# RWKV time mixing on one core: when output tiles are stored and when their buffers are used again

## The chip, the core and the metric

The kernel runs on one core of one Trainium2 chip. The time is the device time of one execution in microseconds, as a median over runs. The profile is of one execution and gives its span, which is a little shorter than the time of the same run (286.8 us of 288.48 us).

## The reference

The inputs are `k` and `v` of shape 16 x 2048 x 256 (batch, time, channel) and per-channel vectors `w` and `u`, all float32. For every batch and channel a state `(aa, bb, pp)` is carried over time:

```python
ww = u + kk
qq = np.maximum(pp, ww)
e1 = np.exp(pp - qq)
e2 = np.exp(ww - qq)
output[b, t, :] = (e1 * aa + e2 * vv) / (e1 * bb + e2 + 1e-08)
ww = pp - w + kk
qq = np.maximum(ww, kk)
e1 = np.exp(ww - qq)
e2 = np.exp(kk - qq)
aa = e1 * aa + e2 * vv
bb = e1 * bb + e2
pp = qq
```

`aa` and `bb` are a decayed sum of `exp(k) v` and of `exp(k)`; `pp` is a running maximum that keeps the exponentials in range. Each output is a quotient of two such sums. Both inputs have to be read once and the output written once: 67.12 MB read and 33.55 MB written.

## The kernel before, in words

**Tiles.** Time is cut into 16 chunks of 128 steps (`NST`), and the 16 batches into 4 groups of four. That gives 64 tiles (`NP`), numbered `n = 4 * chunk + group`. A tile of `k`, of `v` or of the output is 128 partitions (the steps) by 4 batches by 256 channels in float32, 512 KB, and is moved by one DMA.

**One slot.** The main loop (lines 458 to 497) handles one tile per pass, which is called a slot here; slots 0 to 9 run a shorter loop (lines 425 to 445). In slot `n`

- `exps(n)` (L222) lets ScalarE take the exponentials that TensorE prepared in PSUM (`logs`, L203 and L209);
- `round_k(n + 2)` (L193) and `cast_v` (L227) let VectorE copy a loaded `k` or `v` tile into its working form, and give its float32 load buffer back;
- `times_v(n)` (L233) multiplies by `v`;
- for the tile `q = n - 10` (`LAG` is 10), TensorE makes the denominators (`den`, L360), and ScalarE turns them into reciprocals in a float32 output buffer `RD[q]`: `den_log` (L365, a logarithm), then `den_exp` (L368);
- for `qp = n - 11`, TensorE makes the numerators (`num`, L377), and VectorE multiplies them into the same buffer (`mult`, L381). The tile is then complete.

**The state across chunks** is worked on once in four slots, on small tiles: `sums`, `copy_sums`, `turn`, `state_logs`, `state_frames`, `state_scan` (a scan on VectorE, L292), `state_offsets` (L301 to L305), `state_weights` (an exponential on ScalarE, L309), `state_chain`, and `inject`, which writes the new state into the operand ring `EZR` with four small DMAs (L350). `state_offsets(c)` has five element-wise instructions of at most 128 x 64 elements. `E` is the engine of the first three: VectorE in chunks 0, 1 and 15 (`ON_DVE`), GpSimd else. `E2` is the engine of the last two: GpSimd in all chunks but the last.

**Buffers.** All 512 KB tiles share 19 buffers (`BUFS`). At the start 8 of them (`OUTS`) are in the list `free_out`, for outputs, and 11 in the list `free`, for loads. Each entry has the slot from which it may be taken, and `take` takes the earliest. `store(n, slot)` (L385) puts the stored buffer back into `free_out` with the slot `slot + STORED`, and `den_log` takes one there. If fewer than three output buffers will be available in two slots, `loads` moves a load buffer over to the outputs, for good (line 81). `loads` issues `v` and `k` loads (L73, L69), at most nine tiles ahead, while two load buffers are free; with fewer load buffers it gets less far ahead.

**Order.** The order of the instructions on each engine is written out by hand: `K` keeps them in program order. All loads and all stores go through the one queue of SyncE (called SPq in the profile) in program order, and an entry there that waits for its buffer holds back all behind it. Where an instruction takes a buffer before its store has landed, the build adds a wait. The slot numbers of `take` only decide which buffer is taken; they do not make anything wait.

**How late stores are.** In slot `n` the last complete tile is `qp - 1`, with `qp = n - 11`. While loads are left to issue, line 485 allows stores of tiles below `qp - 2 - max(0, n - 18) // 6`: two slots later than possible at first, three from slot 24, and one more every six slots, until they are eight late at slot 54. In each slot in which this number steps, no store is issued. When all loads are issued, the held-back stores go out at once: nine in slot 60. Loads get the bandwidth that the held-back stores leave.

Of the kernel before, what the change touches and what calls it, by code (L numbers as in the profile page):

```python
# [10 lines left out]
ALU = mybir.AluOpType  # L11
# [4 lines left out]
def kernel(  # L16
# [9 lines left out]
    K = tc.keep_in_program_order  # L26
    PE, DVE, SC, POOL, SP = nc.tensor, nc.vector, nc.scalar, nc.gpsimd, nc.sync
# [6 lines left out]
    NP = 4 * NST  # L34
    RING = 12
    BUFS, OUTS = 19, 8
    STORED = 3
    LAG = 10
    RS = 2.0 ** -20
    CAP = 54.0  # L40
# [11 lines left out]
    def rows_of(x, n):  # L52
        c, p = divmod(n, 4)
        return x[4 * p:4 * p + 4, c * TC:(c + 1) * TC, :].rearrange("n t d -> t n d")
# [22 lines left out]
    loaded = 5  # L77

    def loads(slot):
        nonlocal loaded  # L80
        if slot + 2 >= LAG and sum(x <= slot + 2 for x, _ in free_out) < 3:
            free_out.append((slot + 2, take(slot, free)))
        while loaded < NP and loaded - slot < 9 and sum(x <= slot for x, _ in free) >= 2:
            load_v(loaded, slot)
            loaded += 1
            if loaded < NP:
                load_k(loaded, slot)
# [102 lines left out]
    def round_k(n, slot=0):  # L190
        km = consts.tile([128, 4, Dm], F32R, tag=f"km{n % 2}", name="km") if n < 2 else KM[n - 2]
        kr = kr_of.pop(n)
        K(DVE.tensor_copy(km, kr))  # L193
        free.append((slot, kr))
        KM[n] = km

    def logs(n):
        km = KM[n].rearrange("p (i n) d -> p i (n d)", i=2)

        def rows(q):  # L200
            for i in range(2):
                g = 32 * (2 * q + i)
                K(PE.matmul(half(n, q)[:, i, :], CO[g:g + 32, :],  # L203
                            WU[g:g + 32, :].unsqueeze(1).broadcast_to([32, 2, Dm]), start=True, stop=False,
                            tile_position=(g, 0), skip_group_check=True))

        def steps(q):
            for i in range(2):
                K(PE.matmul(half(n, q)[:, i, :], (NLE, NLZ)[q], km[:, i, :], start=False, stop=True,  # L209
                            skip_group_check=True))  # L210

        rows(0)
        rows(1)
        steps(0)
        steps(1)

    def exps(n):
        if n < TURNS:
            for q in range(2):
                K(SC.activation(ez(n)[:, q], half(n, q), ACT.Exp))  # L220
        else:
            K(SC.activation(ez(n)[:, 0:2], PS[:, 0:4, :].rearrange("p (q i) x -> p q i x", q=2), ACT.Exp))  # L222

    def cast_v(n, slot=0):
        vb = vbpool.tile([128, 4, Dm], BF16, tag="vb", name="vb")
        vr = vr_of.pop(n)
        K(DVE.tensor_copy(vb, vr))  # L227
        free.append((slot, vr))
        VB[n] = vb

    def times_v(n):
        vb = VB.pop(n).rearrange("p (i n) d -> p i (n d)", i=2)
        K(DVE.tensor_mul(ez(n)[:, 2:4], ez(n)[:, 0:2], vb.unsqueeze(1).broadcast_to([128, 2, 2, D])))  # L233
# [61 lines left out]
    def state_offsets(c):  # L295
        E = DVE if c in ON_DVE else POOL
        E2 = POOL if c < NST - 1 else DVE
        A, P, F = [x[c % 2] for x in (A_of, P_of, F_of)]
        out = A.rearrange("p h m -> p m h")
        Q = tiny.tile([128, 32, 2], F32, tag="Q", name="Q")  # L300
        K(E.tensor_tensor(Q, P[:, :, 0:2], F[:, :, 1:3], ALU.add))  # L301
        K(E.tensor_tensor(out[:, :, 0:2], Q, P[:, :, 1:3], ALU.subtract))
        K(E.tensor_single_scalar(out[:, :, 2:4], Q, CAP, op=ALU.min))
        K(E2.tensor_single_scalar(out[:, :, 4:6], P[:, :, 1:3], -1.0, op=ALU.mult))
        K(E2.tensor_copy(LL_of[(c + 1) % 2][:, 0, :, 0:1], P[:, :, 2:3]))  # L305

    def state_weights(c):
# [49 lines left out]
    def den(n, bank=DENB):  # L357
        for m, q in (("L", 0), ("Id", 1)):
            for i in range(2):
                K(PE.matmul(bank[:, i, :], mats[m], ez(n)[:, q, i, :], start=q == 0, stop=q == 1,  # L360
                            skip_group_check=True))
# [13 lines left out]
    def num(n, bank, i):  # L375
        for m, q in (("LN", 2), ("IdN", 3)):
            K(PE.matmul(bank, mats[m], ez(n)[:, q, i, :], start=q == 2, stop=q == 3, skip_group_check=True))  # L377

    def mult(n, bank, i):
        rd = RD[n]  # L380
        K(DVE.tensor_mul(rd[:, i, :], bank, rd[:, i, :]))  # L381

    def store(n, slot):
        rd = RD.pop(n).rearrange("p i (n d) -> p (i n) d", n=2)
        K(SP.dma_start(out=rows_of(out, n), in_=rd))  # L385
        free_out.append((slot + STORED, rd))

    later = {}
    for c in range(NST):
        s = 4 * c + 3  # L390
        plan = [(s + 1, "act" if s + 1 < LAG else "recip", copy_sums), (s + 1, "pe", turn),
                (s + 2, "act", state_logs), (s + 2, "mid", state_frames), (s + 2, "scan", state_scan), (s + 2, "scan", state_offsets),
                (s + 3, "recip", state_weights), (s + 3, "chain", state_chain),
                (s + 4, "nums", turn_back), (s + 4, "mid", inject), (s + 4, "mid", state_next)]
        if c == 0:
            plan = [(s + 1, "act", copy_sums), (s + 1, "pe", turn), (s + 1, "pe", state_logs),
                    (s + 1, "round", state_frames), (s + 1, "round", state_scan), (s + 1, "round", state_offsets),
                    (s + 2, "act", state_weights), (s + 2, "round", state_chain),
                    (s + 3, "pe", turn_back), (s + 3, "round", inject), (s + 3, "round", state_next)]
        if c == 1:  # L400
            plan = [(s + 1, "act", copy_sums), (s + 1, "pe", turn), (s + 2, "act", state_logs),
                    (s + 2, "round", state_frames), (s + 2, "round", state_scan), (s + 2, "round", state_offsets),
                    (s + 3, "recip", state_weights), (s + 3, "early", state_chain)] + plan[8:]
        if c == NST - 1:
            plan = []
        for slot, where, f in plan:
            later.setdefault((slot, where), []).append((f, c))

    def small_work(n, where):
        for f, c in later.pop((n, where), []):  # L410
            f(c)
# [35 lines left out]
    stored = 0  # L447

    def inverses(n):
        q, qp = n - LAG, n - LAG - 1  # L450
        if qp >= 0:
            num(qp, NUMB, 1)

        sums(n - 1)
        if n + 1 < NP:
            recip(q, lambda: small_work(n, "recip"))

    for n in range(LAG, NP):

        q, qp = n - LAG, n - LAG - 1  # L460
        if qp >= 0:
            num(qp, NUMB, 0)
        den(q)
        small_work(n, "nums")
        exps(n)
        small_work(n, "act")
        if qp >= 0:
            mult(qp, NUMB, 0)
        small_work(n, "mid")
        if n == LAG:  # L470

            inverses(n)
            small_work(n, "early")
        if n + 2 < NP:
            round_k(n + 2, n)

        if n % 4 in (3, 0):
            cast_v(n, n)
        if n + 1 == NP:
            times_v(n)  # L480
        elif n % 4 < 2:
            cast_v(n + 1, n)
        loads(n)

        while stored < (qp - 2 - max(0, n - 18) // 6 if loaded < NP else qp):
            store(stored, n)
            stored += 1
        if n > LAG:
            inverses(n)
        if qp >= 0:  # L490
            mult(qp, NUMB, 1)
        small_work(n, "scan")
        if n + 1 < NP:
            times_v(n)
            small_work(n, "chain")
            logs(n + 1)
        small_work(n, "pe")
# [53 lines left out]
    n, p = NP - 1, (NP - 1) % 4  # L551
# [38 lines left out]
```

## Time and profile before

| what | value |
|---|---|
| time, median of 3 runs | 289.18 us (288.41 to 289.48) |
| span of the profiled execution | 286.8 us |
| TensorE matmul busy | 261.9 us (91%) |
| VectorE busy | 261.0 us (91%) |
| ScalarE busy | 254.0 us (89%) |
| GpSimd busy | 104.3 us (36%) |
| moved by DMA | 101.54 MB, mean 354 GB/s |
| 512 KB loads and stores, median from issue to landing | 8.0, 8.2 and 7.8 us (`k`, `v`, output) |

Three engines are near 90% busy and the DMA is nearly full too, so no single share tells what bounds the kernel. The stretches have to be read one by one: the first 40 us, in which tiles are loaded and nothing is stored; the slots from about 52 us to 254 us; and the last 33 us, in which only outputs are finished.

### The profile page before, as it was taken

Reading aid. Unit: us, or ns where it says so; the run is one execution under the profiler, and the core shown is the slowest. Engines: PE = TensorE matmul, PEld = TensorE weight load, DVE = VectorE, ACT = ScalarE, POOL = GpSimd, SP = SyncE. Lnnn points to the kernel's source line nnn. Section 1 sums busy time; section 2 is a strip of 40 time slices with the busy share of each in tenths; the row PEclk is TensorE's granted clock in tenths of the full one; section 3 lists DMA queues with packets and bytes.
Section 4 is the critical chain, followed back from the end, with each engine's and each line's share of the span. In section 5 each row is a group of like instructions: output and inputs, shape, how many; then the busy total and the mean of one; then the engine's idle time right before and its main releaser. Section 6 shows DMA issues by size and latency. Waiting matters only on the chain.

```text
span 286.8 us, 5076 instructions
## 1 busy us (share of the span) xinstructions
PE 261.9 (91%) x1694; PEld 119.5 (42%) x1694; DVE 261.0 (91%) x463; ACT 254.0 (89%) x252; POOL 104.3 (36%) x208
## 2 busy tenths in 40 slices
PE   6998896999999999699999999999999999997980
PEld 2444442544444444344444344444454444533430
DVE  4699989999999999699999999999999999987771
ACT  2586768999999998799999999999999999996990
POOL 7000524362535454143445445253445454340000
PEclk9999999999999999999999999999999999999997
DMA  6999999999999999999999999999999999999797
GB/s 220 355 348 349 348 329 349 332 348 355 385 376 383 383 383 373 382 383 379 375 379 377 372 371 384 322 383 371 360 304 380 367 333 370 379 383 369 230 340 253
DMA packets 103586, 101.54 MB, mean 354 GB/s; under 512 B 4284, under 2 KB 103560, under 8 KB 103560
## 3 DMA queue, kind: packets, MB, share of 16 engines
q1 hardware_dynamic: 101336, 100.45, 103.8%
q0 software_dynamic: 1920, 0.50, 0.8%
q8 instruction: 13, 0.21, 0.3%
q10 hardware_dynamic: 304, 0.27, 0.3%
q14 instruction: 13, 0.11, 0.1%
HBM read 67.12 MB, written 33.55 MB: 351 GB/s over the span
## 4 chain that ended last, share of the span: by engine, by line
DVE 38%; PE 21%; DMA 16%; ACT 12%; issue 10%; DVEq 1%; POOL 0%; ACTq 0%; POOLq 0%
DVE EZR L233 15%; DVE buf L381 11%; PE PS L209 8%; PE PS L377 7%; DMA buf<-in_k_dram 6%; DMA out_dram<-buf 6%; ACT buf L368 4%; DVE km L193 4%; ACT buf L365 4%; DVE vb L227 3%; PE PS L203 3%; PE PS L257 3%; ACT EZR L222 2%; DMA EZR<-cb 2%; DMA wuf<-in_u_dram 2%
## 5 line engine op out<-in xcount | busy, mean ns | idle before, releaser
L222 ACT ACTIVATE EZR<-PS 128x2048 bf16<-128x2048 f32 x54 | 101.2, 1875 | 3.6 <-PE PS L209 2.6
L381 DVE TENSOR_TENSOR buf<-PS,buf 128x512 f32<-128x512 f32 x128 | 86.9, 687 | 8.0 <-ACT buf L368 3.6
L233 DVE TENSOR_TENSOR EZR<-EZR,vb 128x2048 bf16<-128x2048 bf16 x64 | 78.2, 1222 | 2.9 <-ACT EZR L220 2.3
L365 ACT ACTIVATE buf<-PS 128x1024 f32<-128x1024 f32 x64 | 65.9, 1029 | 4.6 <-DMA out_dram<-buf 2.8
L368 ACT ACTIVATE buf<-buf 128x1024 f32<-128x1024 f32 (+1 forms) x65 | 67.8, 1048 | 0.9
L350 POOL DMA_DIRECT2D EZR<-cb x60 | 36.8, 619 | 53.2 <-DVE cb L345 46.5
L377 PE MATMUL PS<-EZR,LN 128*128 128x512 bf16 x128 | 48.8, 381 | 6.8 <-DVE buf L381 2.5
L209 PE MATMUL PS<-km,NLE 128*128 128x512 f32 x128 | 47.6, 454 | 1.5 <-DVE km L193 1.5
L377 PE MATMUL PS<-EZR,IdN 128*128 128x512 bf16 x128 | 48.4, 378 | 0.0
L193 DVE CAST km<-buf 128x1024 fp32r<-128x1024 f32 x64 | 43.9, 686 | 1.4 <-DMA buf<-in_k_dram 1.3
L227 DVE CAST vb<-buf 128x1024 bf16<-128x1024 f32 x64 | 43.2, 691 | 0.3 <-DMA buf<-in_v_dram 0.3
L209 PE MATMUL PS<-km,NLZ 128*128 128x512 f32 x128 | 41.0, 403 | 0.0
L360 PE MATMUL PS<-EZR,L 128*128 128x512 bf16 x128 | 38.1, 379 | 1.8 <-DMA EZR<-cb 1.6
L360 PE MATMUL PS<-EZR,Id 128*128 128x512 bf16 x128 | 38.1, 379 | 0.0
L288 POOL TENSOR_TENSOR F<-LL,LL 128x32 f32<-128x32 f32 x13 | 8.2, 631 | 65.5 <-ACT LL L279 65.5
L203 PE MATMUL PS<-WU,CO 32*128 32x512 bf16 x256 | 26.9, 392 | 2.5 <-DVE WU L421 1.6
L257 PE MATMUL PS<-EZR,OH 128*32 128x256 bf16 x512 | 26.2, 277 | 1.1 <-ACT LL L279 1.0
L209 PEld LDWEIGHTS PS<-km,NLZ 128*128 128x128 f32 x128 | 24.6, 192 | 5.7
L220 ACT ACTIVATE EZR<-PS 128x1024 bf16<-128x1024 f32 x20 | 19.4, 1019 | 8.1 <-PE PS L209 8.1
L209 PEld LDWEIGHTS PS<-km,NLE 128*128 128x128 f32 x128 | 19.4, 191 | 16.7 <-issue 13.4
L377 PEld LDWEIGHTS <-IdN 128*128 128x128 bf16 x128 | 12.5, 97 | 22.3 <-issue 20.2
L377 PEld LDWEIGHTS <-LN 128*128 128x128 bf16 x128 | 12.8, 100 | 18.4 <-issue 11.3
(71 smaller groups left out, 201.6 us busy)
## 6 DMA issues: line engine op xcount, KB each, us to landing
buf<-in_k_dram SPq DMA_DIRECT2D x64, 512.0 KB, 8.0
buf<-in_v_dram SPq DMA_DIRECT2D x64, 512.0 KB, 8.2
out_dram<-buf SPq DMA_DIRECT2D x63, 512.0 KB, 7.8
EZR<-cb POOLq DMA_DIRECT2D x60, 8.0 KB, 5.4
out_dram<-buf SPq DMA_DIRECT2D x2, 128.0 KB, 4.4
out_dram<-buf ACTq DMA_DIRECT2D x2, 128.0 KB, 4.5
EZR<-cb SPq DMA_DIRECT2D x4, 8.0 KB, 3.7
wuf<-in_w_dram ACTq DMA_DIRECT2D x1, 8.0 KB
```

Of the source, the lines that this page charges most:

```text
L193: K(DVE.tensor_copy(km, kr))
L203: K(PE.matmul(half(n, q)[:, i, :], CO[g:g + 32, :], WU[g:g + 32, :].unsqueeze(1).broadcast_to([32, 2, Dm]), start=True, stop=False, tile_p ...
L209: K(PE.matmul(half(n, q)[:, i, :], (NLE, NLZ)[q], km[:, i, :], start=False, stop=True, skip_group_check=True))
L222: K(SC.activation(ez(n)[:, 0:2], PS[:, 0:4, :].rearrange("p (q i) x -> p q i x", q=2), ACT.Exp))
L227: K(DVE.tensor_copy(vb, vr))
L233: K(DVE.tensor_mul(ez(n)[:, 2:4], ez(n)[:, 0:2], vb.unsqueeze(1).broadcast_to([128, 2, 2, D])))
L350: K(queue.dma_start(out=EZR[r:r + 1, 2 * q, r0:r0 + 4, :, :].rearrange("o p i (b x) -> o (p i b) x", b=4), in_=cb[x:x + 32, :]))
L360: K(PE.matmul(bank[:, i, :], mats[m], ez(n)[:, q, i, :], start=q == 0, stop=q == 1, skip_group_check=True))
L365: K(SC.activation(RD[n], bank, ACT.Ln, scale=RS))
L368: K(SC.activation(RD[n][:, i, :], RD[n][:, i, :], ACT.Exp, scale=-1.0))
L377: K(PE.matmul(bank, mats[m], ez(n)[:, q, i, :], start=q == 2, stop=q == 3, skip_group_check=True))
L381: K(DVE.tensor_mul(rd[:, i, :], bank, rd[:, i, :]))
```

## The change

The change moves stores earlier, gives a stored buffer more time before it is used again, and moves two small instructions:

1. `STORED` goes from 3 to 4: a buffer is offered to `den_log` four slots behind its store in place of three.
2. The holding back of stores begins at slot 20 and steps every twelve slots: stores are two slots late up to slot 31, three from 32, four from 44 and five from 56. The number of held-back stores at the end is smaller, six being issued in slot 59.
3. In `state_offsets`, the negation (line 304) goes where the first three instructions are. That differs from before in chunks 0 and 1, where it moves from GpSimd to VectorE.

By the pools' rule, the first edits also change which load buffers go over to the outputs: before, one each in slots 31, 37, 43, 49 and 55; after, one each in slots 34 and 58. So more buffers are left for loads in the second half.

```diff
-    STORED = 3
+    STORED = 4
...
-        K(E2.tensor_single_scalar(out[:, :, 4:6], P[:, :, 1:3], -1.0, op=ALU.mult))
+        K((E if E is DVE else E2).tensor_single_scalar(out[:, :, 4:6], P[:, :, 1:3], -1.0, op=ALU.mult))
...
-        while stored < (qp - 2 - max(0, n - 18) // 6 if loaded < NP else qp):
+        while stored < (qp - 2 - max(0, n - 20) // 12 if loaded < NP else qp):
             store(stored, n)
             stored += 1
```

The instructions of TensorE and ScalarE stay the same and in the same order. VectorE gets two instructions more and GpSimd two fewer. On SyncE the same 170 issues stand in another order.

## The prediction

> **What bounds the kernel now.** I read the windows first, cut at starts of the large exponential (L222), which stands once in each slot: slots 18 to 27, 28 to 37 and 38 to 62. The columns are the stretch and its length, busy time of each engine, granted clock, DMA share and GB/s.
>
> ```profile
> core 0: us, PE busy (x) PEld busy (x) DVE busy (x) ACT busy (x) POOL busy (x), PEclk, DMA share, GB/s
> 71.95:111.66 39.71, 38.83 (x261) 17.72 (x260) 39.26 (x67) 39.21 (x38) 18.46 (x34) 1.00 1.09 381
> 111.66:154.54 42.88, 39.16 (x261) 18.17 (x260) 40.01 (x65) 39.67 (x38) 15.44 (x33) 1.00 1.09 380
> 154.54:253.60 99.06, 96.96 (x650) 44.73 (x649) 97.45 (x162) 98.10 (x95) 43.90 (x83) 1.00 1.06 362
> ```
>
> The first ten slots take 39.71 us, the last 25 take 99.06 us: 3.97 and 3.96 us each, with three engines over 96% busy. That is the pace of compute. The ten slots between take 42.88 us for the same work, 3.2 us more than ten times 3.97. The reader should also see the last column. While every slot stores a tile, it moves three tiles of 524,288 bytes; from the first row's 381 GB/s that is 1.573 MB / 381 = 4.13 us, more than 3.97. The DMA is slightly slower than compute there. Late in the run, where before stores only five tiles in six slots, it idles: (381 - 362) GB/s over 99 us is 1.9 MB, 3.6 tiles.
>
> Next the waits, to see who stopped in the slow stretch (total us, times, longest):
>
> ```profile
> DVE buf L381 <- ACT buf L368: 3.6, 7, 0.7
> ...
> DVE buf L381 <- PE PS L377: 3.1, 3, 2.2
> ACT buf L365 <- DMA out_dram<-buf: 2.8, 2, 2.6
> PEld PS L274 <- ACT ts L267: 2.8, 2, 2.5
> ```
>
> ScalarE waits 2.6 us for a store. The 2.5 and 2.2 us of TensorE and VectorE are the same stop handed on. The chain of waits from 104 to 124 us names the store:
>
> ```profile
> 106.82 0.77 ACT buf L368
> 107.59 8.47 DMA out_dram<-buf
> 116.06 0.02 issue
> 116.08 0.02 ACTq L365
> 116.10 0.04 issue
> 116.15 0.04 ACT buf L365
> ```
>
> The logarithm of slot 28 could have begun at 113.54 and began at 116.15. Its buffer had been stored at 107.59, and a store takes 7.8 us at the median to land. Why was the store so late? The SyncE queue in order of time (start, length):
>
> ```profile
> 63.32 0.94 SPq L385 DMA_DIRECT2D out_dram<-buf  x1
> ...
> 96.60 1.21 SPq L385 DMA_DIRECT2D out_dram<-buf  x1
> ...
> 100.67 1.22 SPq L385 DMA_DIRECT2D out_dram<-buf  x1
> 101.98 1.54 SPq L73 DMA_DIRECT2D buf<-in_v_dram  x1
> 103.61 1.23 SPq L69 DMA_DIRECT2D buf<-in_k_dram  x1
> 104.93 1.24 SPq L73 DMA_DIRECT2D buf<-in_v_dram  x1
> 106.27 1.23 SPq L69 DMA_DIRECT2D buf<-in_k_dram  x1
> 107.59 1.23 SPq L385 DMA_DIRECT2D out_dram<-buf  x1
> ```
>
> Each issue takes 1.2 us and more, so SyncE is held by full DMA queues. The store at 107.59 is that of slot 25, whose exponential began at 99.66: the queue runs 8 us, two slots, behind. Two slots of lag plus two of landing make four, while the buffer is used again three slots later. Up to slot 24 it was four in effect, since enough output buffers were free; at slot 24 the first skipped store used one up. The stores at 63.32 (tile 0) and 100.67 (tile 9) give 37.35 / 9 = 4.15 us for three tiles; I use this. It is 0.18 us over the pace of compute. One tile takes 4.15 / 3 = 1.38 us.
>
> **What the skill says.** "DMA: Bandwidth & Descriptors", "Anatomy of one DMA": DMA engines do not wait on semaphores, the issuing sequencer does. The trace agrees: SyncE's own waits include 29.5 us of `k` loads for VectorE's `km` copies, with the stores queued behind. The same page, "Issuing engines are not separate DMA queues": all DMAs interleave on the same 16 engines. The trace agrees in that GpSimd's 8 KB state writes take 5.4 us to land at the median. The page's fabric ceiling of 435 GB/s ("Where 436 GB/s comes from") is not reached: the trace shows 381 in the mixed stretch and 349 with loads alone, and I use these. "GPSIMD Engine Reference", "Engine selection": element-wise work belongs on VectorE. Here the negation takes 0.46 us on GpSimd and 0.22 us on VectorE (chunk 15).
>
> **Negation to VectorE.** Chunk 1, in slot 9:
>
> ```profile
> 41.25 0.46 POOL L304 TENSOR_SCALAR A<-P 128x64 f32<-128x64 f32 x1 [4.26 <-DVE P L292]
> ...
> 41.59 0.22 DVE L303 TENSOR_SCALAR A<-Q 128x64 f32<-128x64 f32 x1
> ...
> 41.60 0.29 POOL L305 COPY LL<-P 128x32 f32<-128x32 f32 x1
> ...
> 41.69 0.74 DVE L227 CAST vb<-buf 128x1024 bf16<-128x1024 f32 x1
> ...
> 41.92 0.36 ACT L309 ACTIVATE G<-A 128x192 f32<-128x192 f32 x1 [0.85 <-POOL LL L305]
> ```
>
> ScalarE waits 0.85 us, ended by GpSimd at 41.89. After, VectorE's negation starts at 41.69 and ends at 41.91, so ScalarE starts at about the same time; GpSimd's copy moves earlier. The cost is two instructions at 0.10 us (start to start of neighbouring small ones) to 0.22 us. In chunk 0 the `k` loads that follow are barely in time (the copy at 39.78 waited 0.91 us for its load), and hide it. In chunk 1 it delays the cast, and all of slots 10 to 12 by 0.1 us, at most 0.2. From slot 31 on the DMA sets the pace for a while, which absorbs it. I take 0.
>
> **`STORED` and the lag, slots 24 to 31.** Removed: the reuse after three slots. Added: the stores that before skipped in slots 24 and 30. The store that stopped ScalarE moves from slot 25 to slot 24, between the `k` load at 103.61 and the `v` load at 104.93. Issued at 104.9, and landing 8.0 us later, it is there at 112.9; slot 28 needs it at 113.54. The 2.6 us go. But the margin is 0.6 us, and every slot with a store loses 0.18: it is gone after three slots.
>
> **Slots 31 to 45.** Then compute waits in each full slot for what the DMA is slower: slots 32 to 35, 4 x 0.18 = 0.7 us. The wait is again L365 behind a store, with TensorE's denominators and numerators queued behind it. Slot 32 skips a store: that returns 1.4 us, two slots after slot 35's buffer. Over twelve slots with eleven stores, the DMA needs 35 x 1.383 = 48.4 us against 47.6, 0.07 us a slot; the margin of 1 to 3.5 us lasts until slot 44, for which I followed the queue tile by tile with these numbers. There loads come in pairs of tiles (moved buffers leave a slot without loads, then two at once) and 0.4 us more are lost. Sum: 1.1 us.
>
> **Slots 45 to 63.** The same reckoning leaves stores 0.5 to 3 us of margin and the last `k` tiles about 3 us. Before, the last `k` load was issued at 240.18 and used at 247.14, 1 us after landing; after, 99 tiles from tile 8's store at 96.60 (landing 104.54) to that load give 104.54 + 99 x 1.383 = 241.5, against a use at 247.14 - 2.1 = 245.0. Fewer load buffers are given up, so the idle DMA time of before is used for the earlier stores. No cost.
>
> **The tail.** ScalarE alternates logarithm and exponential to the end (row 263 to 279 us), each 0.9 us; the stores keep up. Before it, TensorE waits 1.6 us for the last but one state write, issued at 255.67 and landing 5.5 us later. State writes took 5.4 us at the median over the whole run, with full queues and with idle ones, so I leave it. The nine held-back stores become six; they delay nothing today. No change.
>
> **Sum.** Gone: 3.2 us of excess in slots 28 to 37. New: 0.7 + 0.4 = 1.1 us. Gain 2.1 us, less up to 0.1 for the negation: 289.2 - 2.0 = 287.2 us.
>
> **The rivals.**
> - *The whole excess goes* (0.22). At 381 GB/s a full slot is 4.13 us, not 4.15; the margin then loses 0.16 and hardly any wait is left: 289.2 - 3.2 = 286.0 us. For it: the windows; against it: the issue times, which include what small DMAs take.
> - *The wait only moves* (0.22). The DMA sets the time wherever the queue is 8 us behind; compute that no longer stops at slot 28 is stopped in small waits up to slot 58. At 1.40 us a tile, eleven stores in twelve slots need 49.0 us, 0.12 a slot; 27 slots give 3.1 us, all of the gain: 289.2 us. Against it: the last third before is not short of bandwidth.
> - *Slower* (0.08). Stores now compete with loads: the mix falls to 366 GB/s, as in 160 to 170 us of the trace. Then 35 tiles need 50.1 us, 0.21 a slot, 5.7 us over 27 slots: 289.2 + 2.5 = 291.7 us. For it: a `k` margin of only 1 us at the end; against it: those dips came where loads waited for buffers.
>
> **How the numbers follow.** Forecast 0.48 at 287.2 us. The range takes in the first rival with 0.3 us of run-to-run spread, 285.7, and the second, 289.4; only the slower case lies outside, and some edges. The bound of 0.5% is 1.45 us: below 287.7 lie the first rival and most of the forecast, together 0.6; within lie the rest of it and the second, 0.31; slower 0.09.
>
> **What would show it.** Right: no 2.6 us wait at slot 28; waits of L365 behind stores of 0.1 to 0.4 us in slots 31 to 35 and about 44; slots 38 to 62 at 3.97 to 4.0 us with over 370 GB/s. Wrong: `km` copies (L193) waiting for `k` loads late in the run, or larger waits at L365 spread over slots 32 to 58, that is, a DMA slower than 1.39 us a tile.

## The result and the profile after

The changed kernel takes 285.65 us (median of 6 runs, 285.23 to 286.75), the kernel before 289.19 us. The ratio, estimated from all runs and so not the quotient of these medians, is 0.9887, with a 95% interval of 0.9862 to 0.9913. The time is 1.5 us less than the forecast of 287.2 us, and 0.05 us below the low end of its range. The profiled span is 283.5 us against 286.8 us, 3.3 us less.

The same three stretches of the changed kernel, slots 18 to 27, 28 to 37 and 38 to 62 (stretch, length, busy times, clock, DMA share, GB/s):

```profile
core 0: us, PE busy (x) PEld busy (x) DVE busy (x) ACT busy (x) POOL busy (x), PEclk, DMA share, GB/s
72.07:111.79 39.72, 37.95 (x256) 17.71 (x260) 39.27 (x67) 39.21 (x38) 18.43 (x34) 1.00 1.09 382
111.79:152.25 40.46, 37.98 (x256) 18.27 (x260) 39.97 (x65) 39.41 (x38) 16.55 (x33) 1.00 1.09 382
152.25:251.88 99.63, 94.93 (x638) 44.74 (x649) 97.39 (x162) 97.93 (x95) 45.37 (x83) 1.00 1.09 379
```

The middle stretch went from 42.88 to 40.46 us, the last from 99.06 to 99.63. In the last the DMA now moves 379 GB/s in place of 362: it no longer idles. (By the pools' rule the changed kernel moves three load buffers over to the outputs, in slot 46 as well as in slots 34 and 58 named above; before it was five.) TensorE's lower busy time is no gain; 32 of its 1694 matmul records are missing from this trace.

The waits of the changed kernel show the store wait smaller and in more places (total, times, longest):

```profile
ACT buf L365 <- DMA out_dram<-buf: 1.6, 3, 0.7
...
DVE km L193 <- DMA buf<-in_k_dram: 1.2, 3, 0.7
```

ScalarE's own timeline puts them at slots 35, 44 and 49:

```profile
142.29 1.03 ACT L365 ACTIVATE buf<-PS 128x1024 f32<-128x1024 f32 x1 [0.65 <-DMA out_dram<-buf]
...
178.50 1.03 ACT L365 ACTIVATE buf<-PS 128x1024 f32<-128x1024 f32 x1 [0.70 <-DMA out_dram<-buf]
198.69 1.02 ACT L365 ACTIVATE buf<-PS 128x1024 f32<-128x1024 f32 x1 [0.22 <-DMA out_dram<-buf]
```

The sum of the gain: slot 18 starts 0.12 us later, slots 18 to 62 take 1.84 us less (181.65 to 179.81), and what follows slot 63's start takes 1.5 us less. The last part had not been forecast. SyncE's queue at the end, first of the kernel before (start, length):

```profile
258.06 4.10 SPq L385 DMA_DIRECT2D out_dram<-buf  x3
264.38 3.95 SPq L350 DMA_DIRECT2D EZR<-cb  x4
268.43 11.37 SPq L385 DMA_DIRECT2D out_dram<-buf  x9
279.99 2.42 SPq L558 DMA_DIRECT2D out_dram<-buf  x2
```

and of the changed one:

```profile
262.57 2.52 SPq L350 DMA_DIRECT2D EZR<-cb  x4
265.19 12.80 SPq L385 DMA_DIRECT2D out_dram<-buf  x9
278.18 1.40 SPq L558 DMA_DIRECT2D out_dram<-buf  x2
```

The four small DMAs of the last state write (L350) held SyncE for 3.95 us before, 2.52 us now. Behind them stands the store of tile 54. The two halves of its product on VectorE, before and after:

```profile
264.27 1.28 DVE L381 TENSOR_TENSOR buf<-PS,buf 128x512 f32<-128x512 f32 x2
```

```profile
262.46 1.28 DVE L381 TENSOR_TENSOR buf<-PS,buf 128x512 f32<-128x512 f32 x2
```

Before, the store was issued at 268.43, 2.89 us after its product was made; now at 265.19, 1.45 us after. The last DMAs show what comes of it. Their time from issue to landing (line 558), before and after:

```profile
DMA to landing us min/median/max: 4.2/4.5/4.7
```

```profile
DMA to landing us min/median/max: 3.2/3.3/3.4
```

The last output landed 4.86 us after the last product (285.42 against 280.56) before, and 3.42 us after it (282.18 against 278.75) now: 1.44 us less. I call this the tail's length. Compute from the start of slot 63 to the last product is nearly unchanged, 26.96 us before and 26.87 us now.

### The profile page after: what moved, and what is told of

Read it like the earlier page. It is cut to its first block, busy times and chain, and to the rows that moved or that the text cites. A ratio compares the mean times of both kernels' runs of the same rounds, so it can differ in the third digit from the quotient of the medians.

```text
span 283.5 us, 5049 instructions
## 1 busy us (share of the span) xinstructions
PE 256.2 (90%) x1662; PEld 119.5 (42%) x1694; DVE 261.1 (92%) x465; ACT 253.6 (89%) x252; POOL 106.0 (37%) x206
## 4 chain that ended last, share of the span: by engine, by line
DVE 35%; PE 27%; DMA 16%; ACT 9%; issue 9%; DVEq 1%; POOL 0%; ACTq 0%; POOLq 0%
DVE EZR L233 14%; DVE buf L381 11%; PE PS L377 9%; PE PS L209 9%; DMA buf<-in_k_dram 7%; DMA out_dram<-buf 6%; PE PS L257 3%; PE PS L203 3%; ACT EZR L222 3%; ACT buf L365 3%; DVE vb L227 3%; DVE km L193 3%; PE PS L360 2%; ACT buf L368 2%; DMA EZR<-cb 2%
## 5 line engine op out<-in xcount | busy, mean ns | idle before, releaser
L365 ACT ACTIVATE buf<-PS 128x1024 f32<-128x1024 f32 x64 | 65.8, 1028 | 3.4 <-DMA out_dram<-buf 1.6
L350 POOL DMA_DIRECT2D EZR<-cb x60 | 36.7, 617 | 52.0 <-DVE cb L345 44.6
L209 PE MATMUL PS<-km,NLE 128*128 128x512 f32 x128 | 47.6, 454 | 1.8 <-DVE km L193 1.8
L377 PE MATMUL PS<-EZR,IdN 128*128 128x512 bf16 x112 | 42.4, 378 | 0.0
L360 PE MATMUL PS<-EZR,Id 128*128 128x512 bf16 x115 | 35.3, 379 | 0.0
L377 PEld LDWEIGHTS <-LN 128*128 128x128 bf16 x128 | 12.8, 100 | 18.3 <-issue 11.3
```

The source lines that it names most:

```text
L350: K(queue.dma_start(out=EZR[r:r + 1, 2 * q, r0:r0 + 4, :, :].rearrange("o p i (b x) -> o (p i b) x", b=4), in_=cb[x:x + 32, :]))
L365: K(SC.activation(RD[n], bank, ACT.Ln, scale=RS))
```

## The experiments

E1 to E4 ran on one chip, E5 to E8 on another, E9 to E12 on a third; each ratio is to the kernel before on the same chip (288.5 to 288.6 us there). What differs by some tenths between chips is not read from the totals but from the stretches: the start of slot 18 varied from 71.9 to 75.6 us between executions, and part of the reason is seen under E4. In the expectations of E1 and E3, the last product is taken to end 1.1 us earlier than in the others (4.5 us stands for the 3.4 us of the tail's length above).

### Each part alone

E1 sets the reuse gap alone, on the kernel before:

```diff
-    STORED = 3
+    STORED = 4
```

> Only STORED = 4; the stores are held back as in the kernel before. Theory (the loop's gain is the longer reuse gap; the tail's gain is the smaller number of held-back stores): no wait of L365 behind a store is left, slot 63 starts at about 250.6 us (253.6 before), but nine held-back stores reach further into the tail, so the last output lands 6 us or more after the last product; 287.0 us in all, 286.2 to 287.8. Rival (the gain comes from storing earlier, which leaves more buffers for loads and fills the idle DMA time): 288.5 to 289.5 us.

Measured: 287.5 us, ratio 0.9964 (0.9943 to 0.9986). No wait of L365 behind a store is left, and slots 18 to 62 take 179.46 us. Against the theory, late `k` loads now cost something at the end (0.7 us of waits, slots 61 and 62 at 4.46 and 4.26 us), and the tail is 4.35 us long, with its state write holding SyncE for 3.83 us. Two stretches of this run, slots 18 to 37 and 38 to 62:

```profile
73.29:152.75 79.46, 75.86 (x511) 35.81 (x520) 78.71 (x131) 78.54 (x76) 34.86 (x66) 1.00 1.09 381
152.75:252.75 100.00, 94.95 (x637) 44.64 (x648) 97.75 (x161) 98.36 (x95) 44.01 (x83) 1.00 1.07 361
```

The DMA idles in the second as it did before (361 GB/s): with the old hold-back, six buffers go over to outputs, and loads are issued late: the last `k` load at 239.17 us, against 234.35 in the changed kernel. The loop's gain belongs to the reuse gap; the idle DMA and the long tail belong to the hold-back.

E2 changes the hold-back alone, on the kernel before:

```diff
-        while stored < (qp - 2 - max(0, n - 18) // 6 if loaded < NP else qp):
+        while stored < (qp - 2 - max(0, n - 20) // 12 if loaded < NP else qp):
```

> Only the smaller hold-back; a buffer is still used again three slots behind its store. Theory: more stores per slot make the queue later, and the gap of three slots is too short for it: waits of L365 behind stores in many slots, slot 63 at 256 to 257 us, the tail 1.4 us shorter than before; 290.5 us, 289.5 to 291.5. Rival (storing earlier is the gain): 286 to 287 us.

Measured: 290.05 us, ratio 1.0051 (1.0034 to 1.0069): slower than before. Its waits at L365:

```profile
ACT buf L365 <- DMA out_dram<-buf: 5.5, 5, 3.1
```

The largest is 3.1 us, at slot 36; before it was 2.6 us at slot 28. At slot 28 E2 has none: no store is skipped before slot 32, and by the pools' rule the first buffer that is used again after three slots is that of slot 36. The tail is 3.42 us long, as in the changed kernel. So the hold-back alone buys the short tail and pays more for it in the loop. Neither part alone gives the gain of both: -0.4% and +0.5%, against -1.1% together (-1.3% without the negation, E11 below).

### More gap, earlier skips, no skips

E4 gives the changed kernel one slot more before a buffer is used again:

```diff
-    STORED = 4
+    STORED = 5
```

> The changed kernel with STORED = 5. Theory (the 1.3 us of waits left in the loop are store landings within the gap of four slots): those waits go, slot 63 at about 251.0, and the DMA has room in the tail; 284.8 us, 284.2 to 285.4. Rival (the DMA's rate sets the loop, whatever the gap): the waits move to the k loads, 285.2 to 286.5 us.

Measured: 286.51 us, ratio 0.9929 (0.9908 to 0.9951). The mechanism is as the theory has it: no wait behind a store, no late `k` load.

```profile
75.60:254.44 178.84, 170.64 (x1148) 80.54 (x1169) 176.35 (x292) 176.71 (x170) 78.93 (x148) 1.00 1.09 378
```

Slots 18 to 62 at 3.974 us each are the pace of compute. But the total is not better. In the profiled execution (287.41 us, the second slowest of eight) slot 18 began at 75.60, 3.5 us later than in the changed kernel's profile. Of this, 2.9 us arose in slots 10 to 12, where TensorE's granted clock (the figure ahead of the DMA share) was half for a while. The same stretch of E4, then of the changed kernel:

```profile
46.20:53.10 6.90, 5.87 (x23) 2.45 (x24) 4.89 (x9) 3.67 (x3) 2.86 (x6) 0.51 1.11 339
```

```profile
46.20:53.10 6.90, 6.71 (x49) 3.48 (x49) 6.90 (x11) 5.63 (x6) 2.86 (x6) 1.00 1.11 334
```

So the late start explains this one execution. The other seven have no profile, and why the median is 1.7 us above the expected 284.8 us stays open; its interval overlaps that of the changed kernel.

E7 holds back earlier in the changed kernel:

```diff
-        while stored < (qp - 2 - max(0, n - 20) // 12 if loaded < NP else qp):
+        while stored < (qp - 2 - max(0, n - 16) // 10 if loaded < NP else qp):
```

> The changed kernel with the hold-back from slot 16 in steps of ten (six slots late at the end). Theory (the waits left in the loop come from the DMA falling behind before its first skipped store at slot 32): the first skips at slots 26 and 36 keep stores in time, no wait of L365 behind a store, slots 18 to 63 in 178.9 us (179.8 in the profile of the changed kernel), and the tail at most 0.3 us longer: 0.6 us less than the changed kernel beside it. Rival (what the loop saves returns in the tail): the same time as the changed kernel.

E8 is the changed kernel once more, beside it.

> The changed kernel itself, as the measure for the three others on the same chip: 285.3 to 286.5 us, the last output 3.4 us after the last product.

Measured: E7 285.83 us (284.08 to 286.12), ratio 0.9883 (0.9854 to 0.9913); E8 285.44 us (285.20 to 286.35), ratio 0.9893 (0.9870 to 0.9915). Not told apart. E7 has no wait behind a store, takes 178.80 us for slots 18 to 62 and has a tail of 3.41 us, so nothing returned there; its profile began slot 18 at 73.50, with half the granted clock from 47.6 to 51.0 us. Two of its six runs took 284.1 and 284.3 us, and four 285.8 to 286.1. E8 had 0.9 us of store waits, and began at 72.71. What E7 wins in the loop does not show in its median.

The profiles side by side suggest why. In six of the kernels with the changed kernel's loop (the changed one, E5, E6, E8, E9, E11), slot 18 began between 71.88 and 73.11 us and slot 63 between 251.88 and 252.41: starts 1.2 us apart, ends 0.5 us apart. E3, which shares the loop up to slot 58, began at 74.08, had 0.4 us of store waits left, and reached slot 63 at 252.97. It looks as if a late start of compute leaves the DMA less behind, so that the waits behind stores shrink by about as much; no run sets the start by itself. In E4 and E7, where no such wait is left, slot 63 follows the start: 254.44 and 252.30.

E12 takes the hold-back out of the changed kernel:

```diff
-        while stored < (qp - 2 - max(0, n - 20) // 12 if loaded < NP else qp):
+        while stored < (qp - 2 if loaded < NP else qp):
```

> The changed kernel with no hold-back at all: every store two slots late, STORED = 4. Theory (in a full slot the DMA needs 4.15 us and compute 3.97, so without skipped stores the loop runs at the DMA's pace once the gap of four slots is used up): waits of L365 behind stores from slot 31 to the end, slot 63 at 255 to 256 us, the tail 3.4 us behind its last product; 289 us, 288.3 to 290. Rival (the hold-back hardly matters when the gap is four slots): 285.2 to 286.5 us.

Measured: 288.66 us, ratio 1.0001 (0.9990 to 1.0013). All of the gain is gone. Slots 18 to 37 and 38 to 62, and the waits:

```profile
72.76:153.16 80.40, 77.91 (x522) 36.01 (x521) 79.27 (x131) 78.99 (x76) 35.91 (x66) 1.00 1.09 382
153.16:256.91 103.75, 98.45 (x649) 45.30 (x648) 98.54 (x162) 99.12 (x95) 40.39 (x83) 1.00 1.09 382
```

```profile
ACT buf L365 <- DMA out_dram<-buf: 3.6, 12, 0.6
```

Twelve small waits, and 103.75 / 25 = 4.15 us a slot in the last stretch: the time that three tiles take in the DMA, as counted in the prediction. This is the plainest evidence for its central number.

### The tail

E3 was to lengthen the changed kernel's tail by holding three more stores back until then:

```diff
-        while stored < (qp - 2 - max(0, n - 20) // 12 if loaded < NP else qp):
+        while stored < (qp - 2 - max(0, n - 20) // 12 if loaded < NP else qp - 3):
```

> The changed kernel, but when all loads are issued three stores are still held back until the tail. Theory (held-back stores cost the tail 0.5 us each or so): main loop as in the changed kernel (slot 63 at 251.9), the last output lands 5.5 to 6.5 us after the last product in place of 4.5; 287.0 us, 286.5 to 288. Rival (the tail's gain is due to something else, such as the last state write): 285.2 to 286.2 us.

Measured: 285.92 us, ratio 0.9912 (0.9893 to 0.9930); the tail is 3.41 us long. The theory as worded, that held-back stores cost the tail, fell. SyncE is still behind in these slots, so the stores are issued at nearly the times at which they would have been anyway: tile 51 landed 9.1 us after slot 63's start, against 9.3 us in the changed kernel. The number held back in the program does not matter; what is queued when the tail begins might.

E5 and E6 add transfers there that nobody reads, two and four in number:

```diff
+    for n in range(2):
+        K(SP.dma_start(out=take(NP, free), in_=rows_of(k, n)))
     for n in range(stored, q):
         store(n, q + LAG)
     den_exp(q)
```

> The changed kernel with two extra 512 KB loads, read by nobody, in the SyncE queue at the start of the tail. They stand for the transfers that the kernel before left for the tail, where it let the DMA idle for 3.6 tiles in slots 38 to 62. Theory (the tail's gain is that the DMA enters it with less work queued): the last output lands 4.9 us after the last product, as before, in place of 3.4; 1.4 us over the changed kernel beside it. Rival (the tail's gain has another cause, so two tiles more find idle DMA time): 3.4 us as now, the same time.

> As before, with four extra loads. Theory: the slack of the tail is used up by the first two, so two more add nearly their whole 2.8 us: the last output lands about 7.5 us after the last product; 4 us over the changed kernel. Rival: no more than 1 us over it.

Measured: E5 286.18 us, ratio 0.9910 (0.9885 to 0.9936), tail 3.55 us; E6 288.90 us, ratio 1.0003 (0.9990 to 1.0015), tail 3.32 us. They cost 0.7 and 3.5 us over E8, but the time from the last product on hardly changed (3.41 us in E8): this theory too was wrong in what it expected there. In E5 the store of tile 54 was issued at 265.77, 0.47 us later than in E8, and the last output landed 0.49 us later; the last product came 0.34 us later too, which hides most of it in the tail's length. In E6 the transfers delayed compute itself, seen in its waits from 255 us on:

```profile
ACT buf L365 <- PE PS L360: 5.7, 3, 3.0
PEld L360 <- DMA EZR<-cb: 5.6, 2, 3.7
PE PS L360 <- DMA EZR<-cb: 4.7, 2, 3.2
```

The last state write landed at 270.79 in E6, 265.86 in E8, and TensorE waited for it; right after it, from 271.3 to 274.7 us, its granted clock was half, so that this profile, of the slowest of E6's runs (289.61 us), overstates the delay. In the kernel before the write landed at 269.33, in time but for some tenths. So transfers left at the tail's start can cost in two ways; the wait for the state write is one, but not the one at work between the two kernels.

E9 tests the other one, the late issue of the store behind the state write, nearly without bytes:

```diff
     inject(c, SP)
+    for n in range(2):
+        K(SP.dma_start(out=take(NP, free)[0:1, 0, :], in_=k[n, 0:1, :]))
     outputs(q + 1)
```

> The changed kernel with two extra loads of 1 KB each, read by nobody, in the SyncE queue right behind the last state write. They add issue time of about 0.6 us each and nearly no bytes. Theory (the tail was longer before because SyncE, held up at the last state write by full queues, issued the next store late: 2.9 us after its product in place of 1.45): the store of tile 54 is issued 2.6 us or so after its product, the stores behind it drain more slowly than they fill, and the last output lands 4.5 us after the last product in place of 3.4; 1.1 us over the changed kernel, 286.6 us. Rival (the bytes queued ahead did it, not the late issue): 3.4 us, 285.5 us.

Measured: 286.56 us, ratio 0.9919 (0.9889 to 0.9950); 0.9 us over the changed kernel's 285.65, on another chip. The intervals of the ratios overlap, so the reading rests on the profile. SyncE in this run:

```profile
263.06 2.51 SPq L350 DMA_DIRECT2D EZR<-cb  x4
265.62 0.71 SPq L541 DMA_DIRECT2D buf<-in_k_dram  x2
266.44 12.04 SPq L385 DMA_DIRECT2D out_dram<-buf  x9
```

The two tiny loads took 0.71 us in place of 1.2. The store of tile 54 was issued 2.21 us after its product, 0.76 us later than in the changed kernel, and the tail was 4.06 us long, 0.64 us longer. Over all runs:

| run | store of tile 54 after its product, us | tail's length, us | from that store's issue to the last landing, us |
|---|---|---|---|
| changed, E2, E3, E4, E7, E8, E11, E12 | 1.45 to 1.46 | 3.38 to 3.42 | 16.94 to 16.99 |
| E9 | 2.21 | 4.06 | 16.86 |
| E10 | 2.18 | 4.15 | 16.99 |
| E1 | 2.77 | 4.35 | 16.98 |
| before | 2.89 | 4.86 | 16.99 |
| E5 | 1.88 | 3.55 | 16.98 |
| E6 | 3.54 | 3.32 | 19.30 |

The last column is the plainest. In every run but E6, whose compute was held up by more than 4 us, the last output lands 16.9 to 17.0 us after the issue of tile 54's store, whatever the kernel; in E1 and E5 compute was also some tenths late, which shortens their tail as counted from the last product. From that issue on it is the DMA that is behind: in the changed kernel the stores of tiles 54 to 62 land 1.54 us apart (268.33 to 280.68), though the last of them are made 1.86 us apart. The ten tiles (nine stores, and the last tile in four DMAs) take the same time before and after:

```profile
268.43:285.42 16.99, 10.05 (x44) 3.99 (x42) 8.92 (x14) 10.65 (x13) 0.00 (x0) 0.94 0.94 309
```

```profile
265.19:282.18 16.99, 11.27 (x50) 4.67 (x48) 10.22 (x16) 12.08 (x14) 0.00 (x0) 0.94 0.92 309
```

So a delay of tile 54's store is a delay of the end.

### The negation

E10 is the kernel before with line 304 changed, E11 the changed kernel with line 304 put back:

```diff
-        K(E2.tensor_single_scalar(out[:, :, 4:6], P[:, :, 1:3], -1.0, op=ALU.mult))
+        K((E if E is DVE else E2).tensor_single_scalar(out[:, :, 4:6], P[:, :, 1:3], -1.0, op=ALU.mult))
```

> The kernel before with the negation of chunks 0 and 1 on VectorE and nothing else. All theories: no more than 0.2 us either way, 288.4 to 288.9 us where the kernel before has 288.6. ScalarE's wait before L309 in chunk 1 goes from 0.85 us to about 0.7.

> The changed kernel with the negation back on GpSimd. All theories: as the changed kernel, 285.2 to 286.0 us.

Measured: E10 289.15 us, ratio 1.0014 (0.9997 to 1.0032); E11 285.11 us, ratio 0.9870 (0.9839 to 0.9901), where the changed kernel had 0.9887. Both lean towards the negation on VectorE costing about 0.4 to 0.7 us (0.0014 and 0.0017 to 0.0023 in the ratios), and the intervals do not settle it. ScalarE's wait before L309 did not shrink in general: 0.7 us in the changed kernel's profile, but 1.9 us in two waits in E8 and in E10, against 1.1 before and 1.3 in E11.

## Why the prediction was right and where not

- **What bounds the loop**: right. A full slot needs 4.15 us of DMA and 3.97 of compute. Without skips (E12) the last stretch runs at 4.15, and with a longer gap (E4) or earlier skips (E7) the loop runs at 3.97.
- **The 2.6 us at slot 28 go**: right, and due to the reuse gap: E1 has the gain in the loop, while in E2 a larger wait stands at slot 36 in its place.
- **New waits of 1.1 us**: right in kind and nearly in size. Over 3.97 us a slot, slots 28 to 37 lost 0.75 us (0.7 forecast); slots 38 to 62 took 0.57 us more than before (0.4 forecast). They came in fewer, larger pieces: 0.65, 0.70 and 0.22 us at slots 35, 44 and 49, not 0.18 in each of four slots. E4 and E7 remove them, which shows what they were. I had not reckoned with how far they seem to depend on the start of compute.
- **The last `k` load in time**: right. It landed at 242.57 (241.5 forecast) and was used at 245.42 (245.0).
- **The negation costs nothing**: not refuted; a cost of some tenths stays open.
- **The tail does not change**: wrong, and nearly the whole of the 1.5 us between forecast and result. The step that failed is "The nine held-back stores become six; they delay nothing today", with "the stores keep up" before it. I had checked whether ScalarE's chain waited in the tail, which it did not. I had not followed SyncE's queue there: in the kernel before it spent 3.95 us on the last state write, the store behind it went out 1.4 us later than it does now, and the end followed that issue by 16.99 us in both kernels. E9 shows that the late issue alone lengthens the tail, 0.64 us for 0.76; E1, with the old hold-back, keeps most of the long tail, and E2, with the new one, has the short one. E3 shows that it is not the number of stores held back in the program that counts.

The terms of the loop held: 1.84 us gained there against 2.1 forecast. The rival "The whole excess goes" (286.0 us) came nearest in number, but by luck: its mechanism did not hold, since waits behind stores stayed in the loop (1.6 us) and the rest of the gain came from the tail.

What stays open is why the last state write held SyncE for so long. In the kernel before, E1 and E10, where it took 3.2 to 3.95 us, the store issued before it (tile 53) landed 4.35 to 4.99 us after the write's first issue; in the runs with 2.5 us it landed 1.2 to 2.7 us after. That points to transfers still in flight. But E5, with two more transfers of 512 KB ahead of these stores, held SyncE for only 2.94 us. And no version run here is measurably faster than the changed kernel; E7 removes the loop's waits, but its median is no lower.

## What to carry to other kernels

Where DMA and compute are within a few per cent of each other, ask in which stretch each one is the slower: deferring a few stores lets compute run at its pace, but only while the buffers left for loads keep the DMA from idling; what then goes out late is still in flight when the tail begins. A buffer's reuse distance has to cover the issuing queue's lag as well as the landing, here two slots and two. In the tail, follow the issuing queue as well as the engines: four small DMAs ahead of a store moved the end by 1.4 us, because from that store on the DMA was behind until the end.

## What the runs showed of the hardware that was not expected

- An issue on SyncE took 0.37 us late in the tail, where a store landed 3 to 5 us after it, and mostly 1.2 to 1.4 us in the loop, where landing took 8 us. A run of four 8 KB DMAs held everything behind it for 2.5 to 3.95 us.
- GpSimd's small state writes took no less time to land where the DMA idled: in the kernel before, 4.9 us at the median in slots 18 to 37 (380 GB/s), 5.4 us in slots 38 to 62 (362 GB/s). The last one, from SyncE, landed 1.8 to 2.9 us after its issue in the changed kernel and its repeat E8.
- The start of slot 18 varied by 3.7 us between executions of programs whose DMA issues are in the same order up to there. Part of it goes with TensorE's granted clock. In E1, E3, E5 and E7 it was half for 3.4 us between the starts of slots 10 and 13, in E4 for 6.9 us. These three slots took 14.4 to 14.7 us in the four, 16.6 us in E4, and 12.8 to 13.8 us in the nine other profiles. What halves the clock is not shown here. Where a later wait for the DMA absorbs a late start, the total hides it; where that wait is gone (E4, E7), it shows in full.
